# A depthwise convolution moved to TensorE as 64x32 tap matrices, its group norm in that layout, and a new order of the mixer

## The chip, the cores and the metric

The kernel runs on one core of one Trainium2 chip. A core has five engines with their own instruction queues, each worked off strictly in order: TensorE (PE in the profile, its weight loads PEld), VectorE (DVE), ScalarE (ACT), GpSimd (POOL) and SyncE (SP). SP issues all of this kernel's transfers between DRAM and on-chip memory. The metric is device time in microseconds, the median of the runs.

## The reference

One layer on 1024 tokens of 1024 features, in float32. The token mixer projects the normed input to 3072 columns. The first 1024 make a convolution group, the rest an HGRN2 group of four heads:

```python
def _conv_mixer(u_val, u_gate, w_dw, b_dw, gn_gain, gn_bias):
    u = u_val * jax.nn.sigmoid(u_gate)                    # 512 channels
    y = lax.conv_general_dilated(u, w_dw[:, None, :], padding=[(30, 0)],
                                 feature_group_count=512) + b_dw   # 31 causal taps a channel
    # group norm over 8 groups of 64 channels, per token
    return jax.nn.silu(yf * gn_gain + gn_bias)

h = _rms(x, g_pre_mix) * (1.0 + sc_m) + sh_m
p = h @ w_in + b_in
cv = _conv_mixer(p[..., :512], p[..., 512:1024], ...)
hg = _hgrn2(q, fl, i, g, lb, g_out)    # columns 1024 to 3071, 512 each
y = jnp.concatenate([cv, hg], axis=-1) @ w_out
x = x + gt_m * _rms(y, g_post_mix)
```

The channel mixer follows: a norm, an up projection to 4096, squared ReLU, a down projection, a norm and a residual.

## The kernel before

All tiles are 128 partitions wide. A big product is made of three float32r products (high part by high, high by low, low by high), so one column tile of the input projection (128 of the 3072 columns, all 1024 tokens) costs 8 x 3 x 2 = 48 products of 512 columns. A float32 product that is not split appears as two records in the trace.

A class `Weave` sets the order. Streams (Python generators) yield when they would have to wait; `Weave` keeps an estimated clock for each engine, and emits a stream's next instructions when their inputs should be ready. The order on every engine is therefore fixed when the program is built, by the cost formulas in lines 251 to 254.

The stages: an opening (`start`) loads and norms x, computes the first modulation vectors and the first three column tiles (`FIRST`, tiles pf). Then `mixer` (line 1076) runs the other column tiles in the order of `ORDER`, and whatever hangs on a finished tile is woven in between. Then `out_proj`, in which tiles of `EARLY` come first for six of the eight token tiles, and `LATE` after; then the channel mixer (`up`, `down`).

The column tiles are numbered: 0 to 3 conv values, 4 to 7 conv gates, 8 to 11 queries, 12 to 15 forget gates, 16 to 19 the heads' values, 20 to 23 output gates. All but 16 to 19 come out with channels on partitions and tokens along the row; `v_mm` (line 851) computes the heads' values with tokens on partitions, in products of 256 columns.

The convolution has one channel tile of 128 channels at a time. `conv_near` (line 667) runs 20 of the 31 taps on VectorE, each a multiply and add over a whole row into the tile cacc. `conv_far` (line 640) does the other 11 taps on GpSimd, with part of the multiplications on ScalarE. `conv_norm` (line 685) transposes the sum on TensorE (cpt) to tokens on partitions, norms groups of 64 channels, and transposes back (cpb).

Each head runs `head_att` (line 778): seven levels, in each of which TensorE makes a product (pl), VectorE scales three tiles and writes a masked part into the tile att. There is one att tile, so a head starts its levels when the head before has used it up (`att_turn`). `head_state` (to_nat's tn, pS) and `head_out` (po, pot) follow.

Weights arrive by `Loads`: SP loads 512 KB into a stage, ScalarE and VectorE or GpSimd split it. `gate_rows` and `ffn_cols` compute later modulation vectors from in_wada_n, mostly on VectorE.

Of the kernel before, what the change touches and what calls it, by code (L numbers as in the profile page):

```python
# [21 lines left out]
PADW = TAPS - 1  # L22
FF = 4096
NFF = FF // P
NSLOT = 53
# [3 lines left out]
V_BIN, V_BDW, V_GNG, V_GNB, V_GHG, V_LB0, V_LB1, V_GPF, V_WDW = 48, 72, 76, 80, 84, 88, 92, 96, 104  # L29
V_N = V_WDW + 4 * TAPS  # L30
# [7 lines left out]
FIRST = (4, 0, 12)  # L38
ORDER = (5, 8, 13, 9, 1, 6, 16, 2, 7, 14, 21, 10, 20, 3, 15, 18, 23, 11, 22)
# [9 lines left out]
POOL_TAPS, ACT_OF, ACT_TAPS = 11, 2, 1  # L49


EARLY, LATE = (0, 4, 2, 5, 1, 6), (3, 7)
# [3 lines left out]
R0, STAGE, WRING = 12, 3, 6  # L56
SPARE, WOSPARE, HRES = 5, 4, 2
# [5 lines left out]
XRANK, MRANK, RMODS, RFAR, RNEAR, RLOAD, RNORM = 0, 1, 7, 6, 9, 3.5, 1.5  # L63
# [3 lines left out]
class Slots:  # L67
# [3 lines left out]
    def __init__(self, pool, n):  # L71
        self.pool, self.free = pool, list(range(n))
# [3 lines left out]

    def room(self, n):
        return lambda: len(self.free) >= n
# [5 lines left out]
class Slot:  # L84
    def __init__(self, owner, i, dtype):
        self.owner, self.i = owner, i
        t = owner.pool.tile([P, 1024], dtype, tag=f"s{i}", name=f"s{i}", bufs=1)
        if dtype == F32:
            self.f = t
        else:  # L90
            self.r = t

    def release(self):
        self.owner.free.append(self.i)


class Ring:
# [7 lines left out]
    def room(self, n=1):  # L105
        def enough():
            more = n - len(self.items)
            return more <= 0 or (len(self.items) + len(self.lent) + more <= self.n
                                 and len(self.slots.free) >= more + self.spare)
        return enough  # L110

    def next(self):
        self.lent.append(self.items.pop(0) if self.items else self.slots.new(self.dtype))
        assert len(self.items) + len(self.lent) <= self.n
        return self.lent[-1]

    def give(self, item=None):

        item = item or self.lent[0]
        self.lent.remove(item)  # L120
        self.items.append(item)
# [46 lines left out]
class Weave:  # L168
# [16 lines left out]
    def engine(self, eng, key, cost):  # L185
        weave = self

        class Timed:
            def __getattr__(self, name):
                op = getattr(eng, name)  # L190

                def call(*a, **k):
                    weave.spend(key, cost(name, free_size(a[name == "reduce_sum"] if a else k["out"])))
# [53 lines left out]
def block_kernel(ctx: ExitStack, tc: tile.TileContext, x, vecs, masks, rows, vrow, wada_t, wada_n,  # L247
                 win0, win, winv, wout, wup, wdn, out):
# [17 lines left out]
    slots = Slots(big, NSLOT)  # L266
# [6 lines left out]
    def tiny(name, cols=1):  # L273
        return small.tile([P, 8], F32, tag="tiny", name=name, bufs=16)[:, 0:cols]
# [27 lines left out]
    def split(src, hi, lo):  # L302
# [4 lines left out]
        if max(wv.t["G"], wv.now) + n / 460 <= max(wv.t["V"], wv.now) + n / 960 + LO_G:  # L307
# [17 lines left out]
    mhalf = const.tile([P, 8], F32, name="mhalf")  # L325
# [49 lines left out]
    def x_load(n):  # L375
        xn[n] = new()
# [191 lines left out]
    def rest():  # L568
        yield lambda: len(mod_loads) == 4
        srcs = []  # L570
        for j in ORDER:
            srcs += [winv[(j - 16) // 2, i] for i in range(2)] if 16 <= j < 20 else [win[j]]
# [32 lines left out]
    def put_mix(kt, half, fn):  # L605
# [9 lines left out]
        marks.t["mix", kt, half] = wv.now  # L615


    def tap(j, s):
        return col(V_WDW + j * TAPS + PADW - s)

    convs = [dict() for _ in range(4)]
    heads = [dict() for _ in range(4)]

    def conv_gate(j, ps):
        yield room(1)
        u = convs[j]["u"] = new()
        A.activation(u.f, ps, AF.Sigmoid, bias=bcol(4 + j))
        mm.done(ps, "A")
        yield

    def conv_val(j, ps):
        u = convs[j]["u"]
        yield after("A")
        V.scalar_tensor_tensor(u.f, ps, bcol(j), u.f, ALU.add, ALU.mult)
        mm.done(ps, "V")
        yield after("V")
        wv.add(conv_far(j), RFAR)
        wv.add(conv_near(j), RNEAR)

    def conv_far(j):  # L640

        c = convs[j]
        nd = TAPS - POOL_TAPS
        yield room(SPARE + 2)
        c["pacc"] = new()
# [1192 lines left out]
```

## Time and profile before

| what | value |
|---|---|
| median of three runs | 1155.27 us (1154.88 to 1155.27) |
| the profiled execution, its own time | 1161.52 us |
| its span, from the first to the last instruction | 1159.7 us |
| mean granted TensorE clock | 0.971 |
| transfers that SP issues | 353 |

How to read the profile's rows: a group of instructions has its line, engine, operation, the tile written and the tiles read, the shapes and the count, then busy microseconds and the mean duration in nanoseconds, then the idle time of its engine just before it with what ended it. Most operations go through one recording helper (line 194, line 1731 for products), so the tile names tell them apart: s is any of the 53 big tiles. A row of the timeline has the start, the duration, and what ran. A row of the stages has, behind the length, the busy time of each engine with its number of instructions, then the mean granted clock, the busy share of the 16 DMA engines, and GB/s.

### The profile page before, as it was taken

How to read it: one execution, taken by the hardware profiler on the slowest of the kernel's cores; microseconds unless marked ns; L12 is line 12 of the kernel's file. 1: busy time of each engine (PE TensorE's matmuls, PEld its weight loads, DVE VectorE, ACT ScalarE, POOL GpSimd, SP SyncE). 2: the span in 40 equal slices, each digit the busy share in tenths (PEclk: the TensorE clock that was granted, in tenths of full speed). 3: DMA queues.
4: the chain of work that ended last, by engine and by line, in shares of the span. 5: the costliest groups of instructions: out<-in, count | busy, mean ns of one | idle time of the engine just before them, and what ended most of it. 6: DMA issues, size and time to landing. Idle time of an engine off the chain costs nothing.

```text
span 1159.7 us, 14360 instructions
## 1 busy us (share of the span) xinstructions
PE 1090.5 (94%) x5606; PEld 909.5 (78%) x5606; DVE 845.0 (73%) x798; ACT 491.7 (42%) x691; POOL 479.6 (41%) x348
## 2 busy tenths in 40 slices
PE   3899879899998999978999999999999999999996
PEld 3787769787797788857888888888888888888885
DVE  5968988899999986464754986432356969996942
ACT  5643133323433353557544233566543434444520
POOL 6527778756688682484200232223400001304301
PEclk6899889989999999989999999999999999999999
DMA  9423213322311020355467774423666866674801
GB/s 371 165 65 109 74 54 110 127 80 85 92 37 37 26 85 1 117 210 200 145 256 276 293 263 164 135 76 133 220 254 228 319 225 231 246 262 158 323 22 73
DMA packets 50899, 183.96 MB, mean 159 GB/s; under 512 B 5648, under 2 KB 5904, under 8 KB 50832
## 3 DMA queue, kind: packets, MB, share of 16 engines
q1 hardware_dynamic: 50832, 183.05, 44.5%
q8 instruction: 44, 0.72, 0.3%
q14 instruction: 23, 0.19, 0.0%
HBM read 149.47 MB, written 33.55 MB: 158 GB/s over the span
## 4 chain that ended last, share of the span: by engine, by line
PE 54%; DVE 1%; POOL 0%; ACT 0%; DMA 0%; issue 0%; DVEq 0%; POOLq 0%; ACTq 0%
PE pup L1731 26%; PE al L1731 15%; PE be L1731 11%; PE pout L1731 1%; PE pt L1735 1%; DVE s L194 1%; POOL s L194 0%; ACT junk L194 0%; DMA x2d<-s 0%; PE pg L1731 0%; DVEq L1834 0%; POOLq L1834 0%; POOL last_ss L194 0%; POOL fr L194 0%; ACTq L1834 0%
## 5 line engine op out<-in xcount | busy, mean ns | idle before, releaser
L194 POOL TENSOR_TENSOR s<-s,s 128x1024 fp32r<-128x1024 f32 (+9 forms) x164 | 303.7, 1866 | 479.5 <-ACT s L194 443.6
L194 DVE TENSOR_TENSOR s<-s,s 128x1024 fp32r<-128x1024 f32 (+3 forms) x333 | 413.9, 1282 | 80.5 <-ACT s L194 56.1
L194 ACT ACTIVATE s<-s 128x1024 fp32r<-128x1024 f32 (+4 forms) x317 | 298.4, 972 | 298.9 <-DVE s L194 192.1
L1731 PE MATMUL pup<-s,s 128*128 128x512 f32 x1344 | 309.1, 391 | 0.0
L1731 PEld LDWEIGHTS pup<-s,s 128*128 128x128 f32 x1344 | 252.4, 188 | 52.1
L1731 PE MATMUL pj<-s,s 128*128 128x512 f32 (+1 forms) x1200 | 252.1, 366 | 0.0
L1731 PEld LDWEIGHTS pj<-s,s 128*128 128x128 f32 x1200 | 202.4, 193 | 33.0 <-ACT s L194 0.3
L1731 PE MATMUL al<-s,s 128*128 128x512 f32 x768 | 175.6, 390 | 3.1 <-DVE s L194 3.1
L1731 PEld LDWEIGHTS al<-s,s 128*128 128x128 f32 x768 | 143.9, 188 | 34.2 <-DVE s L194 4.3
L1731 PE MATMUL be<-s,s 128*128 128x512 f32 x576 | 131.0, 389 | 0.0
L1731 PEld LDWEIGHTS be<-s,s 128*128 128x128 f32 x576 | 108.1, 188 | 22.5
L1731 PE MATMUL pout<-s,s 128*128 128x512 f32 x384 | 96.4, 401 | 8.4 <-DVE s L194 8.3
L194 DVE SCALAR_TENSOR_TENSOR cacc<-s,vec,cacc 128x1023 f32<-128x1023 f32 (+18 forms) x76 | 96.9, 1275 | 1.1
L1731 PEld LDWEIGHTS pout<-s,s 128*128 128x128 f32 x384 | 71.1, 191 | 23.8 <-DVE s L194 9.2
L194 DVE SCALAR_TENSOR_TENSOR s<-s,c_act,s 128x1024 f32<-128x1024 f32 (+1 forms) x48 | 68.6, 1430 | 19.4 <-DMA s<-in_wada_n 18.0
L194 DVE SCALAR_TENSOR_TENSOR s<-pup,s 128x1024 f32<-128x1024 f32 x16 | 19.6, 1225 | 53.3 <-PE pup L1731 50.4
L194 DVE TENSOR_TENSOR s<-pup,s 128x1024 f32<-128x1024 f32 x24 | 29.3, 1222 | 40.0 <-PE pup L1731 40.0
L194 ACT ACTIVATE s<-s,vec 128x512 f32<-128x512 f32 (+5 forms) x40 | 28.3, 710 | 58.4 <-POOL s L194 58.3
L1731 PEld LDWEIGHTS pl<-s,s 128*16 128x16 f32 (+3 forms) x640 | 34.0, 137 | 21.9 <-issue 15.9
L1731 PE MATMUL pl<-s,s 128*16 128x16 f32 (+3 forms) x640 | 35.9, 222 | 14.8 <-DVE s L194 12.7
L1731 PE MATMUL pf<-s,s 128*128 128x512 f32 x144 | 41.3, 429 | 5.2 <-DVE s L194 3.7
L194 POOL TENSOR_SCALAR s<-s,vec 128x512 f32<-128x512 f32 (+6 forms) x44 | 45.3, 1031 | 0.0
(119 smaller groups left out, 757.1 us busy)
## 6 DMA issues: line engine op xcount, KB each, us to landing
s<-in_wdn SPq DMA_DIRECT2D x72, 512.0 KB, 5.2
s<-in_wup SPq DMA_DIRECT2D x56, 512.0 KB, 5.6
s<-in_wada_n SPq DMA_DIRECT2D x32, 512.0 KB, 3.5
s<-in_win SPq DMA_DIRECT2D x17, 512.0 KB, 3.6
s<-in_x SPq DMA_DIRECT2D x16, 512.0 KB, 6.4
s<-in_wada_t SPq DMA_DIRECT2D x16, 512.0 KB, 9.8
u<-s SPq DMA_DIRECT2D x16, 512.0 KB, 2.9
s<-u SPq DMA_DIRECT2D x16, 512.0 KB, 4.5
```

The lines of the kernel that those rows point to most:

```text
L194: return op(*a, **k)
L1731: return self.te.matmul(out, lhsT=lhsT, rhs=rhs, **k)
L1735: return self.te.transpose(out, in_, identity)
```

## The change

The gate and value columns of the convolution group (G, U) and the heads' values (V) are now all computed with tokens on partitions (`t_mm`): four steps each of 48 products with 512 moving columns. `t_gate` adds the bias and takes the sigmoid, `t_val` adds the bias, multiplies on GpSimd, and SP stores the product to a DRAM tile `udram`, behind 32 rows of zeros.

`conv_input` reads it back into one block tile, `wide`, of four slots. The tokens are cut into 32 blocks of 32; a block's column holds the 64 rows from 32 before the block to its end (row 0 is replaced by ones, which carry the bias). Channels are taken in two halves, each as two groups of rows (partitions 0 to 63 and 64 to 127), so a half takes two reads of 31 rows and two of 32. Then `conv_mm` issues 256 products for each half in two bursts: the stationary operand is the channel's 64x32 tap matrix (made on the host, loaded as in_toep), the moving one its 32 blocks. The result has tokens on partitions again; `conv_evac` copies it out, `conv_norm` norms 1024 columns at once, and `conv_out` turns it back with products by the identity (cpb), which ends in the out projection's input.

Beside this: two attention tiles, so two heads' levels may run at the same time; `FIRST` and `ORDER` bring the first two heads forward, then V, G, U, then the other two heads; `EARLY` and `LATE` of the out projection change; the modulation columns are computed before the gate rows; the ring of split weights has 12 tiles until the last of G, U, V is done and 6 after; the planner's cost formulas for VectorE, ScalarE, GpSimd and products are new.

```diff
-FIRST = (4, 0, 12)
-ORDER = (5, 8, 13, 9, 1, 6, 16, 2, 7, 14, 21, 10, 20, 3, 15, 18, 23, 11, 22)
+TGROUPS = 'GUV'
+FIRST = (12, 8, 13)
+ORDER = (9, 20, 'V0', 'V1', 'V2', 'V3', 'G0', 'G1', 'G2', 'G3', 21, 'U0', 'U1', 'U2', 'U3', 14, 10, 22, 15, 11, 23)
...
-EARLY, LATE = (0, 4, 2, 5, 1, 6), (3, 7)
+EARLY, LATE = (0, 1, 2, 3, 4, 5), (6, 7)
...
-    V = wv.engine(nc.vector, "V", lambda op, n: (0.13 if "scalar" in op else 0.07) + n / 960)
-    A = wv.engine(nc.scalar, "A", lambda op, n: 0.17 + n / 1190)
-    G = wv.engine(nc.gpsimd, "G", lambda op, n: 0.1 + n / (1000 if op == "tensor_scalar" else 460))
+    V = wv.engine(nc.vector, "V", lambda op, n: 0.16 + n / 930)
+    A = wv.engine(nc.scalar, "A", lambda op, n: 0.22 + n / 1190)
+    G = wv.engine(nc.gpsimd, "G", lambda op, n: 0.55 + n / (1350 if op == "tensor_scalar" else 520))
...
-        for s in range(0, TAPS - POOL_TAPS):
-            yield idle("V", NEAR)
-            if s == 0:
-                V.tensor_scalar(acc, uf, tap(j, 0), col(V_BDW + j), ALU.mult, ALU.add)
-            else:
-                V.scalar_tensor_tensor(acc[:, s:], uf[:, 0:T - s], tap(j, s), acc[:, s:], ALU.mult, ALU.add)
...
+    def t_val(s, ps):
+        yield room(1)
+        u = new()
+        V.tensor_tensor(u.f.rearrange("p (a c) -> p a c", c=512), ps.rearrange("p (a c) -> p a c", c=512),
+                        crow_s.f[:, None, H1].broadcast_to([P, 2, 512]), ALU.add)
+        mm.done(ps, "V")
+        yield after("V")
+        G.tensor_tensor(u.f, u.f, sig[s].f, ALU.mult)
+        yield after("G")
+        r0 = CB + 256 * s
+        S.dma_start(udram[r0:r0 + 256, :].rearrange("(a p) c -> p a c", p=P), u.f.rearrange("p (a c) -> p a c", c=512))
...
+    def conv_input():
+        yield slots.gone
+        w = slots.wide().rearrange("p (b c) -> p b c", c=P)
+        for r in range(2):
+            S.dma_start(w[64 * r:64 * r + 1, 0, :], ones[0:1, :])
+            nc.sync.dma_start(w[64 * r:64 * r + 1, 1:, :], ones[1:CB, :])
+        for p in range(2):
+            yield room(4)
+            toeps = [new() for _ in range(4)]
+            for c in range(4):
+                S.dma_start(toeps[c].f, toep[p, c])
+            for r in range(2):
+                for a, n in ((1, CB - 1), (CB, CB)):
+                    src = udram[a:a + T, (2 * p + r) * P:(2 * p + r + 1) * P].rearrange("(b i) c -> i b c", i=CB)
+                    nc.sync.dma_start(w[64 * r + a:64 * r + a + n, :, :], src[0:n])
+                wv.spend("S", 3.0)
+            yield wv.t["S"] + DLAT
+            yield from conv_mm(p, w, toeps)
...
+    def conv_mm(p, w, toeps):
+        for q in range(2):
+            yield acc.free
+            ps = acc.take(ps_acc("cv"))
+            for i in range(16):
+                m = 16 * q + i
+                for c in range(4):
+                    for r in range(2):
+                        rows = slice(64 * r, 64 * r + 64)
+                        TE.matmul(ps[CB * c:CB * c + CB, 512 * r + CB * i:512 * r + CB * i + CB],
+                                  lhsT=toeps[c].f[rows, CB * m:CB * m + CB], rhs=w[rows, :, CB * c + m],
+                                  start=True, stop=True, us=0.03)
...
     def head_att(j):
-        yield lambda: att_turn[0] == j
+        yield lambda: att_turn[0] >= j - 1
         hd = heads[j]
+        att = atts[j % 2]
...
-    def v_mm(j0):
...
+    def t_mm(kind, s):
+        if s == 0:
+            yield loads[0].has(4)
+            tws[:] = [loads[0].get() for _ in range(4)]
+        yield mm.free
+        ps = ps2("pt" + kind)
+        for k in range(KT):
+            w = tws[k // 2]
+            for q in range(2):
+                tsl = slice((2 * s % 4 + q) * P, (2 * s % 4 + q + 1) * P)
+                mm_half(TE, ps[:, HALF[q]], [t[:, tsl] for t in h_halves(k)[s // 2]],
+                        [t[:, HALF[k % 2]] for t in w], k == 0, k == KT - 1)
```

Where instructions stand. On SP, before, this is the end of the mixer's loads: in_win are a column tile's weights, in_wout the out projection's.

```order
L194 DMA s_762<-in_win 128x1024
L194 DMA s_217<-in_win 128x1024
L194 DMA s_762<-in_wout 128x1024
L194 DMA s_217<-in_wout 128x1024
L194 DMA s_3171<-in_wout 128x1024
```

On SP, now, behind the last store to udram: the ones for the second group of rows, the first half's tap tiles (in_toep) and the first two of its four reads into wide.

```order
L233 DMA wide<-ones 1x16x8
L709 DMA wide<-ones 1x31x128
L233 DMA s_2125<-in_toep 128x1024
L233 DMA s_2126<-in_toep 128x1024
L233 DMA s_2127<-in_toep 128x1024
L233 DMA s_2128<-in_toep 128x1024
L718 DMA wide<-udram 31x32x128
L718 DMA wide<-udram 32x32x128
```

The row of 31 and the row of 32 repeat for the second group of rows, and after a load of in_rows and one of in_win the whole group from in_toep on repeats for the second half of the channels. Before, no transfer of SP has other than 128 rows.

On PE, before, this is where the first channel tile's convolution comes back: pj are projection tiles, pg a gate row, cpt the transposes of the convolution's sum, among products of 256 columns for the heads' values.

```order
L1731 MATMUL pj_1153<-s_107,s_634 128x512 x2
L1731 MATMUL pj_1153<-s_106,s_635 128x512 x2
L1731 MATMUL pj_1153<-s_108,s_634 128x512 x2
L1731 MATMUL pj_1153<-s_109,s_634 128x512 x2
L1731 MATMUL pj_1153<-s_108,s_635 128x512 x2
L1731 MATMUL pg<-s_1188,ones_r 128x512
L1731 MATMUL pg<-s_1189,ones_r 128x512
L1735 MATMUL cpt<-msk,s_712 128x128 x4
L1731 MATMUL pj_1275<-s_501,s_94 128x256
```

On PE, now, the end of the two column tiles (14 and 10) that follow U's last step, and the first tap products (cv), two for each of the four tap tiles in turn.

```order
L1835 MATMUL pj_2169<-s_109,s_762 128x512 x2
L1835 MATMUL pj_2169<-s_111,s_761 128x512 x2
L1835 MATMUL pj_2169<-s_112,s_761 128x512 x2
L1835 MATMUL pj_2169<-s_111,s_762 128x512 x2
L1835 MATMUL cv<-wide,s_2125 32x32 x2
L1835 MATMUL cv<-wide,s_2126 32x32 x2
L1835 MATMUL cv<-wide,s_2127 32x32 x2
L1835 MATMUL cv<-wide,s_2128 32x32 x2
```

Between U's last step and the first cv stand 96 projection products; after the first burst of 128 tap products come two of pg and 6 of pj, then the second burst, then two of pg and 60 of pj, then the second half's first burst, 12 of pj and its second. Nothing of the convolution stands on PE before this place.

More of the change, by code (lines that the diff above doesn't have):

```diff
@@ L614, in put_mix @@
         yield from split(full, hi.r[:, sl], lo.r[:, sl])
[L615 to L621, printed above, removed]
+        for n in range(4):
+            marks.t["mix", kt, half * 4 + n] = wv.now
     heads = [dict() for _ in range(4)]
[L624 to L634, printed above, removed]
+    udram = dram.tile([CB + T, 512], F32, name="udram")
+    crow_s = new()
+    S.dma_start(crow_s.f, crow.broadcast_to([P, 1024]))
+    sig = [None] * 4
+    ys = [None, None]
+    u_rows = [0]
+    def t_gate(s, ps):
+        sig[s] = slots.new_last()
+        V.tensor_tensor(sig[s].f.rearrange("p (a c) -> p a c", c=512), ps.rearrange("p (a c) -> p a c", c=512),
+                        crow_s.f[:, None, H0].broadcast_to([P, 2, 512]), ALU.add)
@@ new lines, in block_kernel, with conv_evac @@
+    acc = Banks(wv, 1)
+    def conv_evac(p, q, ps):
+        pv = ps.rearrange("p (r i b) -> p r i b", r=2, i=16)
+        if q == 0:
+            yield room(2)
+            ys[p] = [new(), new()]
+        yield lambda: ys[p]
+        for s in range(2):
+            yv = ys[p][s].f.rearrange("t (b r q i) -> t q r i b", r=2, q=2, i=16)
+            for r in range(2):
+                A.activation(yv[:, q, r], pv[:, r, :, 16 * s:16 * s + 16], AF.Copy)
+        acc.done(ps, "A")
+        yield after("A")
+        if q:
+            for s in range(2):
+                wv.add(conv_norm(p, s), RNORM)
@@ new lines, in block_kernel, with conv_out @@
+    normed = {}
+    def conv_out(s):
+        yield room(2)
+        z, sz = new(), new()
+        for h in range(2):
+            yield aux_free
+            pb = ps1("cpb")
+            for b in range(4):
+                bb = (s % 2) * 8 + 4 * h + b
+                for p in range(2):
+                    TE.matmul(pb[64 * p:64 * p + 64, b * P:(b + 1) * P], lhsT=ys[p][s // 2].f[:, bb * 64:bb * 64 + 64],
+                              rhs=ident, start=True, stop=True, us=0.11)
+            yield after("PE", 0.2)
+            pv = pb.rearrange("p (b c i) -> p c b i", c=4, i=CB)
+            zv = z.f[:, HALF[h]].rearrange("p (c b i) -> p c b i", c=4, i=CB)
+            for c in range(4):
+                A.activation(zv[:, c], pv[:, c], AF.Identity, bias=col(V_GNB + c), scale=col(V_GNG + c))
+            done1(pb, "A")
+        A.activation(sz.f, z.f, AF.Sigmoid)
+        yield after("A")
+        V.tensor_tensor(z.f, z.f, sz.f, ALU.mult)
+        sz.release()
+        yield after("V", 0)
+        yield room(2)
+        hi, lo = mix[s % 2, s // 2] = pair()
+        yield from split(z.f, hi.r, lo.r)
+        z.release()
+        for n in 2 * s, 2 * s + 1:
+            for k in range(4):
+                marks.t["mix", k, n] = wv.now
@@ L885, in head_state @@
     def head_state(j):
         hd = heads[j]
-        yield lambda: ("vh", 0) in hd and ("vh", 1) in hd
+        yield lambda: all(("vh", s) in hd for s in range(4))
         v, f = hd["v"].f, hd["f"].f
@@ L1008, in gate_rows @@
         acc.release()
[L1009 to L1010 removed]
+        gs = new()
+        g = gs.f
         yield ring.room()
@@ L1065, in load_wo @@
     def load_wo(k):
-        yield lambda: len(slots.free) >= WOSPARE + 2 and bool(stage.room()())
+        yield lambda: slots.left() >= WOSPARE + 2 and bool(stage.room()())
         hi, lo = pair()
```

319 lines of the change are left out of this document (161 added, 158 removed).

## The prediction

> **What bounds the kernel now.** I read the page's first part, then the busy times by stage, then what the TensorE waited for.
>
> ```profile
> PE 1090.5 (94%) x5606; PEld 909.5 (78%) x5606; DVE 845.0 (73%) x798; ACT 491.7 (42%) x691; POOL 479.6 (41%) x348
> ...
> core 0: us, PE busy (x) PEld busy (x) DVE busy (x) ACT busy (x) POOL busy (x), PEclk, DMA share, GB/s
> 0.00:76.68 76.68, 55.44 (x263) 45.11 (x263) 51.70 (x89) 43.53 (x81) 36.84 (x48) 0.82 0.60 227
> 76.68:554.84 478.16, 439.98 (x2726) 373.01 (x2725) 396.77 (x398) 190.28 (x342) 322.57 (x238) 0.96 0.26 88
> 554.84:1159.70 604.86, 595.11 (x2623) 491.40 (x2621) 396.49 (x313) 257.92 (x269) 120.21 (x62) 1.00 0.57 206
> ```
>
> PE is busy 94% of the span, so this is a TensorE kernel almost everywhere. The stages are the opening, then everything from the first later projection (76.68) to the steady up projection (554.84), then the rest of the channel mixer. The change lies in the second. There PE is idle 478.16 - 439.98 = 38.2 us, and at a mean clock of 0.96 some 0.04 x 478 = 19 us more go into slow cycles. So at most about 57 us can be won. What those waits are:
>
> ```profile
> PE pl L1731 <- DVE s L194: 16.9, 12, 3.5
> PE pout L1731 <- DVE s L194: 8.3, 1, 8.3
> PE pt L1735 <- POOL s L194: 3.8, 1, 3.8
> PE po L1731 <- DVE s L194: 2.9, 2, 2.7
> PE pot L1735 <- ACT s L194: 2.5, 2, 1.9
> PE pl L1731 <- DVE gsf L194: 2.0, 1, 2.0
> PE pg L1731 <- DVE s L194: 1.3, 1, 1.3
> ```
>
> The columns are total us, times, longest. Mostly a head's next level (pl) waits for VectorE, which in this stage is busy 396.8 of 478 us, largely with convolution taps. The waits inside the mixer (all but pout and pt) come to 25.6 us.
>
> **What is removed.** The taps on VectorE and GpSimd, and the conv's transposes:
>
> ```profile
> L194 DVE SCALAR_TENSOR_TENSOR cacc<-s,vec,cacc 128x1023 f32<-128x1023 f32 (+18 forms) x76 | 96.9, 1275 | 1.1
> ...
> L194 POOL TENSOR_TENSOR s<-s,s 128x512 f32<-128x512 f32 x48 | 73.5, 1532 | 14.4 <-ACT s L194 10.5 <-DVE s L194 2.1
> ...
> L1735 PE MATMUL cpb<-msk,s 128*128 128x128 f32 x32 | 4.9, 274 | 0.0
> L1735 PE MATMUL cpt<-msk,s 128*128 128x128 f32 x32 | 4.7, 274 | 0.0
> ```
>
> VectorE sheds 97 us, GpSimd 80 additions, twenty for each of four channel tiles, of some 1.5 us by the row's mean (120 us), PE 9.6 us of transposes. VectorE and GpSimd are off the path except where a head's level waits for them, so their saving counts only through those waits. VectorE gets back some 20 us: eight reads of a projection's result of 1.22 us (the first row below), sixteen of a quarter that size, and group norm on 1024 columns.
>
> ```profile
> L194 DVE TENSOR_TENSOR s<-pup,s 128x1024 f32<-128x1024 f32 x24 | 29.3, 1222 | 40.0 <-PE pup L1731 40.0
> L194 POOL TENSOR_TENSOR s<-s,s 128x1024 f32<-128x1024 f32 x4 | 11.2, 2798 | 18.0 <-DVE s L194 18.0
> ```
>
> With two attention tiles, two heads' levels alternate, and each level has projection work of another head's step before it. I let the 25.6 us of mixer waits shrink to 5, half of pout's 8.3 stay, pt's 3.8 stay, and 15 of the 19 us of slow clock go, since a slow stretch follows a wait. Gain: 20.6 + 4 + 15 = 40 us. Bounds: 57 if nothing waits, 20 if half of it stays. The later order of the modulation loads, the two weight-ring sizes and the out projection's new EARLY are covered by the same PE work; without that cover they are part of the low bound.
>
> **What PE gets.** Rates first:
>
> ```profile
> 338.43 8.88 PE L1731 MATMUL pj<-s,s 128*128 128x256 f32 x72
> ...
> 405.01 3.51 PE L1731 MATMUL po<-s,s 128*128 128x128 f32 x30
> ...
> 442.40 0.70 PE L1731 MATMUL pl<-s,s 128*16 128x16 f32 x64
> 443.03 0.66 PE L1735 MATMUL cpt<-msk,s 128*128 128x128 f32 x4
> ...
> 446.84 0.70 PE L1731 MATMUL pl<-s,s 128*32 128x32 f32 x32
> 447.47 4.40 PE L1731 MATMUL pout<-s,s 128*128 128x512 f32 x18
> ...
> 451.80 1.15 PE L1731 MATMUL pl<-s,s 128*64 128x64 f32 x16
> 452.87 1.65 PE L1731 MATMUL pout<-s,s 128*128 128x512 f32 x6
> ...
> 476.98 27.48 PE L1731 MATMUL pout<-s,s 128*128 128x512 f32 x120
> ```
>
> A 512-column product costs 27.48/120 = 0.229 us, a 256-column one 8.88/72 = 0.123. The value projection turns 384 of the latter into 192 of the former: 47.4 - 44.0 = 3.4 us less. Gate and value columns of the conv group keep 384 products of 512 columns.
>
> The tap products, 512 with 32 stationary and 32 moving columns, are not in the trace. The nearest are pl's (a float32 product is two records): 32 of 16 columns take 443.03 - 442.40 = 0.63 us, 0.020 each, on four 32-row strips of the result in turn; 16 of 32 columns 0.63 us, 0.039 each, on two strips; 8 of 64 columns 1.07 us, 0.134 each. The tap products use four strips and two halves of the rows, so I take 0.03, 15 us in all; bounds 10 (0.020) and 69 (0.134). The 64 products that turn the conv back (cpb) cost between a transpose, 4.9/32 = 0.153, and a po, 3.51/15 = 0.234: 10 to 15 us, I take 11. PE's sum: -3.4 - 9.6 + 15 + 11 = **+13 us** (7 to 71). Without the new wait, the change is worth 40 - 13 = 27 us.
>
> **The new wait.** cv, the first tap product, stands in PE's queue after 96 projection products. It needs the block tile "wide", which SP reads back from DRAM: for each half of the channels two reads of 31 partitions x 32 x 128 and two of 32. Everything behind cv on PE waits with it. How the queue cuts a transfer:
>
> ```profile
> DMA packets 50899, 183.96 MB, mean 159 GB/s; under 512 B 5648, under 2 KB 5904, under 8 KB 50832
> ...
> u<-s SPq DMA_DIRECT2D x16, 512.0 KB, 2.9
> ...
> vec<-in_vecs SPq DMA_DIRECT2D x1, 114.0 KB, 2.1
> ...
> 20.00:40.00 20.00, 14.80 (x63) 11.16 (x64) 16.69 (x25) 10.63 (x21) 16.18 (x21) 0.71 1.00 397
> ```
>
> The issues in the DMA view add up to 353, all of 128 rows. 353 x 128 = 45184 row packets and 353 x 16 = 5648 tiny ones make exactly the queue's 50832. So a transfer is cut by rows into 16 equal shares, each closed by a tiny packet. 31 rows have no equal shares but 31 or one, and there are 16 engines: I expect one engine to move the whole 31 x 32 x 512 B = 508 KB. The last row has all 16 engines busy (share 1.00) at 397 GB/s, 24.8 GB/s each. By bytes one such read takes d = 508/24.8 = 20.5 us. Its 992 packets of 512 B are smaller than any big transfer's here. From vec (8 packets of 912 B per engine, 2.1 us) to u<-s (8 of 4096 B, 2.9 us) a packet grows 0.1 us for 3184 B, 0.13 us for 4096; one engine's full packet at 24.8 GB/s lasts 0.165, which leaves some 0.036 fixed, so 0.052 for 512 B and d = 52. If a small packet cost as much as a full one, d were 164; but vec's 2.1 us, less some 1.6 in which nothing moves (below), leave only 0.06 us for each of its packets, which bounds d at about 60. Spread over 16 engines d is 1.3. I take **d = 28**, nearer to the byte end, because the other is a difference of two noisy landings.
>
> The Trainium skill, "DMA: Bandwidth & Descriptors", section "Why a DMA increments its semaphore by 16 and not by 1", says that the number of engines is the largest up to 16 that divides the slowest dimension of both sides, and that 127 partitions get a single engine. The count of 5648 agrees with it for 128 rows; no run so far shows 31. By it the sum is the forecast's, and if it did not hold, that of rival (1).
>
> The price, from the end of the last value product at 0: VectorE's add 1.2, GpSimd's product 2.8, then four 512 KB tap tiles at 397 GB/s, 5.3: the reads start at 9.3, with the store (2.9) landed by then. Two reads on one engine and some 1.6 us to land (2.9 less 1.3 of moving): ready at 2d + 11. PE arrives at 96 x 0.229 = 22.0: a stall of 2d - 11. The second half reads into the same tile and must wait for cv's second burst: 2 x 3.8 + 0.5 + 6 x 0.229 = 9.5 us after the first; ready at 9.5 + 2d + 1.6. PE's cover is 60 products, so it arrives at 9.5 + 0.5 + 13.7 = 23.7: a stall of 2d - 12.6. Together 4d - 23.6 = 88 us at d = 28. The out projection now starts with the four conv tiles, whose group norm is about a dozen operations of some 1.2 us behind the last tap burst; 114 projection products (26 us) stand between on PE and cover it. Two gaps as long as these also restart the clock cold:
>
> ```profile
> 512.72 2.93 PE L1731 MATMUL pout<-s,s 128*128 128x512 f32 x6 [8.26 <-DVE s L194]
> ```
>
> Six products took 2.93 instead of 1.38 us, so 1.5 us each, 3 together.
>
> **The sum** goes against the profiled execution's own 1161.5 us (span 1159.7): 1161.5 - 27 + 88 + 3 = 1225.5. The median of the runs is 1155.3, 0.54% lower: **1219 us**. The break-even lies at 4d - 20.6 = 27, d = 12 us: as soon as two engines share a read evenly (10 us) the change wins.
>
> **The rivals.**
> (1) The reads are spread over the engines. Then four reads of 1.3 us make the first half ready at 9.3 + 5.2 + 1.6 = 16.1, before PE at 22.0, and the second at 9.5 + 5.2 + 1.6 = 16.3, before 23.7: nothing stalls, and it is 1161.5 - 27 = 1134.5, or 1128 us: faster. For it: every transfer of the trace is spread. Against: all of them have 128 rows. Chance 0.20; its own range 1110 to 1145.
> (2) Spread, but the alternating heads still wait: 25 of the 40 us do not come, 1153 us. For it: each level still needs three VectorE operations and a mask before the next. Against: VectorE has a quarter less to do. Chance 0.05.
> (3) Spread, but the array does not overlap the tap products: 0.134 instead of 0.03 each, 54 us more, 1182 us. For it: half-width pl costs that. Against: pl of 16 and 32 columns. Chance 0.05.
> The forecast, one engine, has 0.70; its own range goes from d = 20.5 with the whole 40 us won and no extra PE work (1161.5 - 40 + 58 + 3, 1176) to d = 45 with 13 won (1161.5 - 13 + 156 + 3, about 1300).
>
> **How the numbers follow.** Faster by over 0.2% (which is about what a measurement of this kernel tells from no change): 0.20 of (1), 0.03 of (2). Same: 0.02 of (2). Slower: 0.70 + 0.05. The range from 1118 to 1290 takes in the forecast's but its far tail, and two thirds of (1): some 0.13 is left out.
>
> **What would show it.** The tiny packets of the DMA line: 16 for each spread transfer and one for each read of 31 rows. In the waits: cv waiting twice for a DMA of wide, 45 and 43 us, and those reads landing 28 and 56 us after issue. The tap bursts of 128 taking 3.8 us each. pl's 16.9 us on VectorE down to a few. If cv waits for nothing, my d is wrong and (1) holds; if cv runs for 17 us per burst, (3).

## The result, and the profile after

The changed kernel takes **1284.05 us** (median of 4 runs, 1281.47 to 1287.83) against 1155.27 us before: ratio 1.1107, 95% interval 1.1067 to 1.1147. It is slower, as forecast, and inside the range, but by 129 us where 64 were forecast.

The page of the changed kernel, its busy line, the granted TensorE clock in tenths (40 equal slices of 32 us), its DMA line and a queue of instructions (packets, MB, share):

```profile
PE 1107.0 (86%) x6508; PEld 915.2 (71%) x6508; DVE 720.7 (56%) x717; ACT 471.3 (37%) x671; POOL 289.6 (23%) x198
...
PEclk6999999999558578899999999999999999999999
...
DMA packets 61597, 195.04 MB, mean 152 GB/s; under 512 B 6134, under 2 KB 14388, under 8 KB 61524
...
q8 instruction: 51, 0.84, 0.3%
```

VectorE shed 124 us (845.0 to 720.7) and GpSimd 190 (479.6 to 289.6), and yet TensorE is busy for 86% of the span instead of 94%. TensorE's idle time went from 1159.7 - 1090.5 = 69.2 to 1281.5 - 1107.0 = 174.5 us. Busy times by stage:

```profile
core 0: us, PE busy (x) PEld busy (x) DVE busy (x) ACT busy (x) POOL busy (x), PEclk, DMA share, GB/s
0.00:79.00 79.00, 57.47 (x268) 45.94 (x268) 50.60 (x87) 43.77 (x82) 40.09 (x50) 0.83 0.59 220
79.00:677.69 598.69, 455.37 (x3623) 378.37 (x3623) 270.44 (x319) 169.63 (x321) 125.39 (x84) 0.87 0.28 88
677.69:1281.50 603.81, 594.21 (x2621) 490.92 (x2619) 399.69 (x311) 257.94 (x270) 124.12 (x64) 1.00 0.59 207
```

The opening and the last stage are nearly as before (they took 76.7 and 604.9 us). The stage between took 478.2 and takes 598.7 us: 120.5 of the 121.8 us lost lie there. What TensorE waits for in it (columns as before: total us, times, longest):

```profile
PE cv L1835 <- DMA wide<-udram: 82.5, 3, 32.4
PE cv L1835 <- issue: 37.0, 5, 28.3
...
PE pl L1835 <- DVE s L233: 12.0, 6, 4.6
PE pout L1835 <- DVE s L233: 4.4, 1, 4.4
```

The tap products wait for 82.5 + 37.0 = 119.5 us. All other idle time is 174.5 - 119.5 = 55.0 us, 14.2 less than before, and busy time is 16.5 us more: 119.5 - 14.2 + 16.5 = 121.8, the growth of the span. So without the waits of cv the change would still not have won anything. The timeline of TensorE around the taps (start, us, engine, what, count, and in brackets the wait ahead and what ended it):

```profile
288.59 21.92 PE L1835 MATMUL pj<-s,s 128*128 128x512 f32 x96
338.78 0.28 PE L1835 MATMUL cv<-wide,s 64*32 64x32 f32 x2 [28.27 <-issue]
371.50 2.01 PE L1835 MATMUL cv<-wide,s 64*32 64x32 f32 x170 [32.44 <-DMA wide<-udram]
376.86 1.14 PE L1835 MATMUL cv<-wide,s 64*32 64x32 f32 x84 [3.35 <-issue]
...
386.13 13.79 PE L1835 MATMUL pj<-s,s 128*128 128x512 f32 x60
418.63 0.28 PE L1835 MATMUL cv<-wide,s 64*32 64x32 f32 x2 [18.71 <-DMA wide<-udram]
450.22 2.59 PE L1835 MATMUL cv<-wide,s 64*32 64x32 f32 x226 [31.31 <-DMA wide<-udram]
454.43 0.51 PE L1835 MATMUL cv<-wide,s 64*32 64x32 f32 x28 [1.61 <-issue]
```

Each half waits twice: its first product (two records) needs rows 0 to 63 of the block tile, the next rows 64 to 127. The four big waits are 110.7 us; the first is put down to issue, but in the run with divided reads below the wait at the same place is put down to the reads. The other four (3.35, 1.61 and two more of 1.54 and 2.25) stand in the middle of a burst, whose first products have already read from all rows and all four tap tiles: 8.75 us. And what SP issues there:

```profile
301.29 60.46 SPq L718 DMA_DIRECT2D wide<-udram x4
...
385.64 55.87 SPq L718 DMA_DIRECT2D wide<-udram x4
```

The two reads of 31 rows of a half land one after the other. From 301.29 to 338.78 are 37.5 us, less 5.3 for the tap tiles queued ahead (2 MB at 397 GB/s) 32.2; then 371.50 - 338.78 = 32.7; in the second half, counted from 385.64, 33.0 and 31.6. That is **d = 32.4 us** for a read of 31 rows, in the mean. SP itself stands still for most of it.

### The profile page after: what moved, and what is told of

Read it like the earlier page. It is cut to its first block, busy times and chain, and to the rows that moved or that the text cites. A ratio compares the mean times of both kernels' runs of the same rounds, so it can differ in the third digit from the quotient of the medians.

```text
span 1281.5 us, 15966 instructions
## 1 busy us (share of the span) xinstructions
PE 1107.0 (86%) x6508; PEld 915.2 (71%) x6508; DVE 720.7 (56%) x717; ACT 471.3 (37%) x671; POOL 289.6 (23%) x198
## 2 busy tenths in 40 slices
DMA packets 61597, 195.04 MB, mean 152 GB/s; under 512 B 6134, under 2 KB 14388, under 8 KB 61524
## 3 DMA queue, kind: packets, MB, share of 16 engines
q1 hardware_dynamic: 61524, 194.03, 43.8%
## 4 chain that ended last, share of the span: by engine, by line
PE 70%; DMA 10%; DVE 8%; SPq 5%; issue 3%; POOL 2%; ACT 2%; DVEq 0%; POOLq 0%; ACTq 0%
PE pup L1835 23%; PE al L1835 14%; PE be L1835 10%; DVE s L233 8%; DMA wide<-udram 6%; PE pout L1835 5%; SPq L718 5%; PE pj L1835 4%; PE ptG L1835 3%; PE ptV L1835 2%; PE pl L1835 2%; DMA s<-in_wada_n 2%; POOL s L233 2%; PE pf L1835 1%; ACT s L233 1%
## 5 line engine op out<-in xcount | busy, mean ns | idle before, releaser
L233 ACT ACTIVATE s<-s 128x1024 fp32r<-128x1024 f32 (+2 forms) x317 | 304.5, 993 | 375.0 <-DVE s L233 202.7
L233 POOL TENSOR_TENSOR s<-s,s 128x1024 fp32r<-128x1024 f32 (+3 forms) x85 | 191.0, 2254 | 714.6 <-ACT s L233 514.4
L1835 PE MATMUL cv<-wide,s 64*32 64x32 f32 x1024 | 12.8, 245 | 119.5 <-DMA wide<-udram 82.5
L1835 PE MATMUL pj<-s,s 128*128 128x512 f32 x432 | 106.1, 405 | 0.0
L1835 PEld LDWEIGHTS cv<-wide,s 64*32 64x32 f32 x1024 | 11.5, 124 | 121.8 <-issue 121.4
L1835 PEld LDWEIGHTS pj<-s,s 128*128 128x128 f32 x432 | 84.3, 197 | 19.2 <-issue 0.7
L233 DVE SCALAR_TENSOR_TENSOR s<-s,c_act,s 128x1024 f32<-128x1024 f32 (+1 forms) x48 | 56.5, 1177 | 45.3 <-DMA s<-in_wada_n 43.6
L233 ACT ACTIVATE s<-cv 128x256 f32<-128x256 f32 x16 | 7.9, 651 | 141.0 <-PE cv L1835 141.0
L233 DVE SCALAR_TENSOR_TENSOR s<-pj,vec,s 128x1024 f32<-128x1024 f32 x7 | 9.0, 1281 | 87.9 <-ACT s L233 87.9
L233 DVE TENSOR_TENSOR s<-pup,s 128x1024 f32<-128x1024 f32 x24 | 29.3, 1222 | 46.0 <-PE pup L1835 45.8
L1835 PE MATMUL ptV<-s,s 128*128 128x512 f32 x192 | 47.3, 396 | 0.0
```

Source lines behind the costliest of these rows:

```text
L233: return op(*a, **k)
L1835: return self.te.matmul(out, lhsT=lhsT, rhs=rhs, **k)
```

## The experiments

In the last columns of this table: cv's waits for data and those put down to issue, all other idle time of TensorE (span less busy less these two), and its busy time, all in us of the profiled execution. "On" is the kernel that a run was edited from. The ratio compares medians with runs of the kernel before that were made beside each run (1158.9 to 1160.0 us for e1 to e13). The profiled execution is a single one: in e9 it is the shortest of ten, 4.8 us under the median, so differences of a few us between two rows can be chance.

| run | on | ratio to before | span | cv, DMA | cv, issue | other idle | busy |
|---|---|---|---|---|---|---|---|
| before | | 1 | 1159.7 | | | 69.2 | 1090.5 |
| after | before | 1.1107 [1.1067, 1.1147] | 1281.5 | 82.5 | 37.0 | 55.0 | 1107.0 |
| e1 reads 16 + 15 | after | 1.0302 [1.0266, 1.0337] | 1192.7 | 14.8 | 14.5 | 56.5 | 1106.9 |
| e3 16-KB rows | e1 | 1.0184 [1.0159, 1.0208] | 1180.4 | 9.9 | 10.0 | 53.8 | 1106.7 |
| e5 taps in pieces | e3 | 1.0123 [1.0100, 1.0147] | 1175.4 | 11.3 | 5.5 | 55.0 | 1103.6 |
| e6 one head at a time | e3 | 1.0121 [1.0083, 1.0158] | 1170.5 | 10.5 | 9.4 | 47.0 | 1103.6 |
| e8 taps later | e6 | 1.0144 [1.0120, 1.0168] | 1174.5 | 0.9 | 10.3 | 66.7 | 1096.6 |
| e9 taps in halves | e6 | 1.0051 [1.0033, 1.0069] | 1159.8 | 11.1 | 3.2 | 48.0 | 1097.5 |
| e7 both | e6 | 1.0075 [1.0053, 1.0097] | 1163.1 | 1.1 | 1.1 | 58.9 | 1102.0 |
| e10 odd and even rows | e6 | 1.0063 [1.0037, 1.0088] | 1166.2 | 6.8 | 9.6 | 50.2 | 1099.6 |
| e11 halves, odd and even | e9 | 1.0026 [1.0012, 1.0041] | 1160.4 | 6.2 | 3.4 | 51.9 | 1098.9 |
| e12 tap tiles early | e11 | 1.0011 [0.9996, 1.0027] | 1156.2 | 0 | 7.5 | 51.4 | 1097.3 |
| e13 taps in quarters | e12 | 1.0054 [1.0040, 1.0068] | 1162.4 | 1.2 | 1.8 | 54.9 | 1104.5 |

### Does one engine carry a read of 31 rows?

Two edits of the changed kernel. The first divides the 31 rows:

```diff
-                for a, n in ((1, CB - 1), (CB, CB)):
+                for a, n in ((1, 16), (17, 15), (CB, CB)):
```

> The change, with each read of 31 rows cut into one of 16 rows and one of 15, the bytes and the packets unchanged. Theory A (a read of 31 rows runs on one DMA engine): the reads spread over 16 and 15 engines and land within some 8 us, PE's waits for wide fall from 119.5 us to under 10, and the time falls from 1284 to between 1150 and 1175 us. Tiny packets: 16 for each read of 16 and of 32 rows, 15 for each of 15. Theory B (packets of 512 bytes scattered over DRAM are slow in themselves, on however many engines): the same packets wait as long, 1275 to 1290 us. The prediction's rival without the wait would be at 1128 us.

Its tap bursts in the timeline:

```profile
320.96 0.28 PE L1835 MATMUL cv<-wide,s 64*32 64x32 f32 x2 [8.18 <-DMA wide<-udram]
327.81 2.00 PE L1835 MATMUL cv<-wide,s 64*32 64x32 f32 x170 [6.57 <-DMA wide<-udram]
334.11 1.14 PE L1835 MATMUL cv<-wide,s 64*32 64x32 f32 x84 [4.29 <-issue]
```

The same bytes, and 90 us of cv's waits (119.5 to 29.3) are gone. The tiny packets rise from 6134 to 6254: four reads that had one each now have 16 + 15, which is 4 x 30 = 120 more. So the 31 rows were one engine's. But A's waits of under 10 us and its time of 1150 to 1175 us were missed: the kernel takes 1194.36 us, 3% more than before, and the product that needs the last of the half's reads starts 24.4 us after SP issued the first (303.42 to 327.81).

The second edit leaves the 31 rows on one engine, and takes them from 16 KB that lie together in DRAM, so that only the size of the pieces differs (the convolution then gets other tokens' values):

```diff
+                    if n < CB:
+                        src = udram[256 * r:256 * r + 256, :].rearrange("(i a) c -> i (a c)", a=8)
+                        nc.sync.dma_start(w[64 * r + a:64 * r + a + n, :, :].rearrange("i b c -> i (b c)"), src[0:n])
+                        continue
```

> The change, with each read of 31 rows taken from a contiguous part of the DRAM tile (31 rows of 16 KB each, so other tokens' values are convolved): the same bytes in large packets, still 31 rows. If one engine carries it and small packets cost the rest, a read takes 508 KB / 24.8 GB/s = 20.5 us instead of some 32.5, PE's waits for wide are about 70 us, the time about 1236 us. If the engine is as slow with large packets, 32.5 us each and 1284 us stay. If the scattered source were all of the cost (theory B), the waits vanish and the time is 1150 to 1175 us.

```profile
333.13 0.28 PE L1839 MATMUL cv<-wide,s 64*32 64x32 f32 x2 [20.66 <-issue]
357.84 2.00 PE L1839 MATMUL cv<-wide,s 64*32 64x32 f32 x170 [24.42 <-DMA wide<-udram]
...
395.65 0.28 PE L1839 MATMUL cv<-wide,s 64*32 64x32 f32 x2 [10.56 <-DMA wide<-udram]
417.38 2.60 PE L1839 MATMUL cv<-wide,s 64*32 64x32 f32 x226 [21.45 <-DMA wide<-udram]
```

One run: 1249.5 us, where 1236 was expected. A read now takes 357.84 - 333.13 = 24.7, 417.38 - 395.65 = 21.7 and, in the second half's first (issued at 370.83), 24.8 us, near the 20.5 us of the bytes alone. So of the 32.4 us some 22 to 25 come from 508 KB on one engine and 8 to 11 from cutting them into 992 packets of 512 B.

### What do the reads still cost when they are shared?

From here on the conv input lies in DRAM by channel group, token within its block, and block, so that every row read back is one piece of 16 KB:

```diff
-    udram = dram.tile([CB + T, 512], F32, name="udram")
+    udram = dram.tile([P, 33 * P], F32, name="udram")
+    uw = udram.rearrange("(g i) (b c) -> i g b c", g=4, c=P)
...
+        for a in range(2):
+            for b in range(4):
+                S.dma_start(uw[:, :, 1 + 8 * s + 4 * a + b, :],
+                            u.f[CB * b:CB * b + CB, HALF[a]].rearrange("i (g c) -> i g c", c=P))
...
+                for a, n in ((1, 16), (17, 15), (CB, CB)):
+                    i0, b0 = (2 * p + r) * CB + a % CB, a // CB
+                    nc.sync.dma_start(w[64 * r + a:64 * r + a + n, :, :].rearrange("i b c -> i (b c)"),
+                                      udram[i0:i0 + n, b0 * P:b0 * P + T * P // CB])
```

> The conv input is stored in DRAM by channel group, token within the block, block, so that each row that is read back is one piece of 16 KB, and the 31 rows are read as 16 and 15. The stores become pieces of 512 B (32 issues in place of 4). Same computation. Theory A (where 16 engines share a read and its packets are large, nothing of the read-back is left on the path, and heads 2 and 3 waited in the earlier run because cv came later than the order had been planned for): cv waits for DMA fall from 14.8 us in the run with 16 and 15 rows to under 2, the waits inside the heads (pl, pout, cpb, 15 us after the taps there) fall to under 8, and the time is 0.985 to 1.000 of the kernel before. Theory B (the order of the heads after the taps is itself what makes PE wait, whatever the reads do): cv's DMA waits go, but the 15 us after the taps stay, and the ratio is 1.005 to 1.020, 1.0302 less some 15 to 25 us. Theory C (the prediction's gain of 27 us without the wait holds): 0.975 to 0.98.

cv's waits fall by another 9.4 us (29.3 to 19.9), the span by 12.3. Not all of this is the layout's: `Weave` now puts 114 projection products ahead of the first burst instead of 96, some 4 us more cover. The gain of 27 us (C) is not there. A is wrong as well: cv still waits 9.9 us for data. B has the ratio, 1.0184, but not its reason, since the DMA waits did not go. Two edits of later kernels show what cv still waits for. One, on e6 (next part), reads the odd and the even rows in place of the lower and the upper:

```diff
-                for a, n in ((1, 16), (17, 15), (CB, CB)):
+                for a, n, st in ((1, 31, 2), (2, 29, 2), (CB, CB, 1)):
```

> As e6_one_head_at_a_time, but the 31 rows are read as the 16 odd and the 15 even partitions instead of the lower 16 and the upper 15. In e6 the reads of a half (2 MB) landed 15 to 18 us after issue, where 397 GB/s would take 5.3. Theory A (rows that go into neighbouring partitions share a way into SBUF, so that a piece of 16 neighbours is slower than 16 rows spread over 32 partitions): the reads land 3 to 6 us earlier, cv's DMA waits fall from 10.5 to 5 to 7 us and the time by 3 to 6 us. Theory B (the 16-KB rows, or the traffic beside them, set the rate): landing and time as in e6, within 2 us.

The DMA view (issues, size, median us from issue to landing), first of e6, then of e10:

```profile
wide<-udram SPq DMA_DIRECT2D x4, 512.0 KB, 14.4
wide<-udram SPq DMA_DIRECT2D x4, 256.0 KB, 9.3
wide<-udram SPq DMA_DIRECT2D x4, 240.0 KB, 12.8
```

```profile
wide<-udram SPq DMA_DIRECT2D x4, 512.0 KB, 11.2
wide<-udram SPq DMA_DIRECT2D x4, 256.0 KB, 7.5
wide<-udram SPq DMA_DIRECT2D x4, 240.0 KB, 9.1
```

The reads land 2 to 4 us earlier and cv waits 6.8 instead of 10.5 us for them, as A has it. The ratios, 1.0121 and 1.0063, touch in their intervals; 4 us of the difference are busy time, which A does not explain. The edit spreads the rows in DRAM as well as over the partitions, so that the way into SBUF is the cause is not shown.

The other edit, on e9 with these reads (e11, below), loads the first half's four tap tiles after the second value projection instead of ahead of the reads, and tells `Weave` 5 instead of 3 us for each group of reads, so that cv keeps its place:

```diff
+        if u_rows[0] == 2:
+            wv.add(toep_load(), RCONV)
...
-                wv.spend("S", 3.0)
+                wv.spend("S", 5.0)
```

> As e11, and the four tap tiles of the first half (2 MB) are loaded after the second value projection instead of ahead of the reads, so that nothing stands before the reads in the DMA queue; the recorder is told 10 us of SP's time for a half's reads, which leaves 57 projection steps ahead of the first burst, as in e9 and e11. Theory A (the first half's wait is queueing behind the 2 MB of tap tiles, 5.3 us at 397 GB/s): the first half's DMA waits of some 7 us in e10 fall to under 2, and the time is 3 to 6 us under e11's, ratio 0.994 to 0.998, faster than the kernel before. Theory B (the reads' own rate sets it): waits as in e11, time within 2 us.

The reads land after 6.0 to 8.1 us, and cv waits no more for data. A is right about the wait. The time, though, is only 0.15% lower than e11's, with intervals that overlap, and misses A's range. The waits for data fell by 6.2 us, those put down to issue rose by 4.1 (3.4 to 7.5); a new wait at cpb was made up by shorter ones elsewhere (other idle 51.9 to 51.4):

```profile
PE cpb L1856 <- ACT s L233: 9.1, 3, 4.8
PE cv L1856 <- issue: 7.5, 5, 3.1
```

### Do two heads in turn help?

```diff
-        yield lambda: att_turn[0] >= j - 1
+        yield lambda: att_turn[0] >= j
```

> As e3_blocked_layout, but a head's levels start only when the head before is through, as in the kernel before, so that the two attention tiles are never worked on in turn. Theory A (the turn of two heads fills PE's waits for a level, as the prediction has it): 5 to 20 us slower than e3_blocked_layout, with more waiting at pl. Theory B (with VectorE relieved, a head alone hardly waits, and the two heads' operations only get in each other's way on VectorE): equal within 3 us or faster.

e6 is faster than e3: 1.0121 against 1.0184, other idle 47.0 against 53.8 us. The waits of pl on ScalarE fall from 5.8 to 1.6 us, those on VectorE only from 3.0 to 2.6. A, the prediction's view, falls. B's reason, that two heads get in each other's way on VectorE, is not shown, since the shorter waits are ScalarE's; the times show that one head at a time is no worse, and probably better, since the intervals barely part.

### What are the waits in the middle of a burst?

> As e3_blocked_layout, and each burst of 128 tap products is cut in four pieces with projection products between them. Theory A (the gaps of 1.5 to 5.4 us in the middle of a burst, put down to issue, come because 256 records of 12 ns each use up PE's instructions faster than new ones arrive): with 64 records at a time the gaps go, and the run is 4 to 9 us faster than e3_blocked_layout. Theory B (the gaps belong to the reads or to the clock, not to the length of the burst): they are as long as in e3_blocked_layout, and the two times agree within 3 us.

The edit is an empty `yield` after every fourth step of a burst. It put other products between the pieces in some bursts only; the first stayed whole, 152 + 102 records with a gap of 2.24 between. Gaps fell from 10.0 to 5.5 us and the time by 0.6%, within A's 4 to 9 us, but long gaps stayed. That did not decide it. But the timeline of e3 says where the gaps stand:

```profile
326.19 1.82 PE L1839 MATMUL cv<-wide,s 64*32 64x32 f32 x152 [6.24 <-DMA wide<-udram]
330.30 1.30 PE L1839 MATMUL cv<-wide,s 64*32 64x32 f32 x102 [2.29 <-issue]
331.53 3.82 PE L1839 MATMUL pj<-s,s 128*128 128x512 f32 x12
335.29 0.33 PE L1839 MATMUL cv<-wide,s 64*32 64x32 f32 x13
336.56 1.50 PE L1839 MATMUL cv<-wide,s 64*32 64x32 f32 x128 [0.95 <-issue]
340.29 1.46 PE L1839 MATMUL cv<-wide,s 64*32 64x32 f32 x115 [2.23 <-issue]
```

From one gap to the next are 102 + 12 + 13 = 127 records, then 128. In the changed kernel the gaps of a burst stand 255, 383 and 255 records apart, two and three times as far. Each record is a weight load and a product, so 128 are 256 instructions. The page's instruction queue moved 0.84 MB in 51 packets, 16.5 KB each, or 64 B for each of 256. Its packets are TensorE's: 6508 products and as many weight loads are 50.8 times 256, and the 5606 of the kernel before are 43.8 times, where its page has 44 packets. So the bursts were cut in halves of 128 records, this time with a time ahead of which the second half is not placed:

```diff
                                   start=True, stop=True, us=0.03)
+                if i % 8 == 7 and i < 15:
+                    yield wv.now + 0.5
```

> As e6_one_head_at_a_time, but each tap burst of 128 products (256 records) is cut in two, with at least six projection products (1.4 us) and mostly more between the halves. In e3 and e6 the issue gaps stand 127 to 128 records apart (x102, x12, x13 between two of them, then x128), which is 256 instructions with the weight loads, 16 KB at 64 B each, as large as the packets of the instruction queue on the page (51 packets, 0.84 MB). Theory A (PE's instructions come in blocks of 256, and a block of tap products is used up in 1.5 us, faster than the next one comes): the gaps shrink from 9.4 us to under 5, since each block now holds projection products too, and the run is 3 to 6 us faster than e6. Theory B (the gaps come from the length of a burst in some other way, such as the clock or the result banks): no gap is left inside a piece of 128 records, and they do not stand 128 apart. Theory C (they hang on the reads): as in e6.

```profile
321.73 1.53 PE L1841 MATMUL cv<-wide,s 64*32 64x32 f32 x128
326.59 1.52 PE L1841 MATMUL cv<-wide,s 64*32 64x32 f32 x128
...
360.42 0.98 PE L1841 MATMUL cv<-wide,s 64*32 64x32 f32 x75
363.44 0.81 PE L1841 MATMUL cv<-wide,s 64*32 64x32 f32 x53 [2.05 <-issue]
```

cv's gaps fall from 9.4 to 3.2 us (a further 1.3 now stands at pj), and the ratio from 1.0121 to 1.0051, with separate intervals. That is 8 us by the medians, more than A's 3 to 6; busy time, which A does not speak of, is 6.1 us less as well. Inside a piece of 128 there can still be one gap, where a block ends there (x75, x53). A holds, and B, by which a piece has none, falls. With quarters of 64 records:

> As e12_tap_tiles_early, but the bursts are cut in four pieces of 64 records with at least six projection products (1.4 us) between them, the tap tiles are loaded after the third value projection, and a half's reads are told as 6 us, so that 54 projection steps stand ahead of the first burst. Theory A (a block of 256 instructions takes some 3.7 us to come, 1.5 us of taps and a gap of 2.2 us): two pieces and two stretches of projection last 4.3 us and more, so cv's issue waits of 7.5 us go to under 2, and the ratio to the kernel before is 0.994 to 0.998, faster. Theory B (the waits only change their place, as cpb's 9.1 us did in e12): issue waits fall, other waits in the mixer rise, ratio 0.999 to 1.002.

The issue waits fall from 7.5 to 1.8 us, as A says. The time does not follow: it rises to 1.0054, past B's range. Most of the rise is no wait at all: busy time is 7.2 us more (1097.3 to 1104.5), other idle time 3.5. The tap tiles are loaded later here and the bursts stand elsewhere too, so the cut alone was not tried. cpb waits 8.0 us for VectorE in place of 9.1 for ScalarE, and pout 9.0 us in all in place of 5.5:

```profile
PE cpb L1856 <- DVE s L233: 8.0, 2, 6.5
PE pout L1856 <- ACT s L233: 5.3, 1, 5.3
```

### Is it only a matter of where the bursts stand?

Before e11 to e13 came the plain remedy on e6: `wv.spend("S", 7.0)` in place of 3.0, which puts the bursts later in TensorE's order; and then this together with e9's halves.

> As e6_one_head_at_a_time, but the recorder is told that the reads of a half take 14 us of SP's time instead of 6, so that it writes the tap bursts later into PE's order: 18 more projection products and two pd ahead of the first burst (some 5 us), and the second half some 27 products later. Theory A (the 10.5 us in which cv still waits for its reads are only a matter of where the burst stands): the DMA waits of cv fall from 10.5 to under 4 us, the time falls by 5 to 8 us from e6's, the issue waits of 9.4 us stay. Theory B (other work is pushed behind by the same amount, and the heads or the out projection wait instead): cv's DMA waits fall, other waits rise by as much, time within 3 us of e6's.

> Both edits of e8 and e9 on top of e6: the 16-KB layout, one head at a time, reads told at 7 us each, bursts cut in two. If the two are independent, the cv waits of 19.9 us fall to under 7 and the time lies 10 to 14 us under e6's, at 0.998 to 1.004 of the kernel before: what the shorter waits in the heads win (22 us in e6) is then about what PE's added work costs (13 us) and what is left of cv's waits. If other work becomes late instead, 1.005 to 1.012.

Waits of e8:

```profile
PE cv L1839 <- issue: 10.3, 5, 2.8
PE pS L1839 <- ACT s L233: 8.5, 1, 8.5
PE cpb L1839 <- DVE s L233: 4.9, 1, 4.9
PE tn L1843 <- DVE s L233: 4.6, 1, 4.6
...
PE cv L1839 <- DMA wide<-udram: 0.9, 1, 0.9
```

B holds: cv's DMA waits go from 10.5 to 0.9 us, and the other idle time from 47.0 to 66.7. In e7 it is the same with a pd that waits 10.0 us for ScalarE: ratio 1.0075 and not better than e9's 1.0051.

> e9_taps_in_halves with the reads of e10_reads_odd_even: both edits on e6. If they add up, cv's DMA waits (11.1 us in e9) fall by some 4 to 6 us, the issue waits stay near e9's 3.2, and the ratio to the kernel before is 1.0051 less 0.004 to 0.006: 0.999 to 1.001. If the earlier reads only move the wait elsewhere, as with e8, 1.003 to 1.007.

e11, with the reads of e10 on e9, comes to 1.0026: DMA waits 11.1 to 6.2 us, half of the gain expected from the sum, and between the two ranges expected. The best of all, e12, equals the kernel before; none of the runs beats it.

## Why the prediction was right in its direction and wrong in its size

The new wait came as forecast, from the same cause. Three terms of the sum were mis-sized: the wait for the reads (88 us, measured 119.5), TensorE's busy time with its slow clock (1 us more, measured 16.5), and the waits in the heads (24.6 us less, measured 14.2).

**One engine for 31 rows: right.** The forecast named 16 tiny packets for a shared transfer and one for a read of 31 rows. Counted out, of the 379 transfers that SP issues now 373 shared ones x 16 = 5968, six transfers of 31 rows (four reads, two of ones) with one each, and 160 pieces of data that are themselves under 512 B (128 rows of the vectors, 400 B now, and 32 of the first ones row) make 6134. With 16 for each read of 31 rows it would be 6224. The Trainium skill, "DMA: Bandwidth & Descriptors", section "Why a DMA increments its semaphore by 16 and not by 1", gives the largest number of engines up to 16 that divides the count of rows, so one for 31, a prime, and 15 for 15. Here 31 rows agree, with 32.4 us for 508 KB, and 16 and 15 rows agree with 120 more tiny packets. Rivals (1), (2) and (3) all had the reads shared, and fall with it.

**d: mechanism right, size too small.** 28 us was taken, between 20.5 by bytes and 52 by packets; it measured 32.4. The choice leaned to the byte end for being better founded; e2 shows both parts, 22 to 25 us of bytes and 8 to 11 of packets. By 4d - 23.6 the stalls would be 106 us; they were 110.7. The first half's were 60.7 instead of 2d - 11 = 53.8, because its reads could start only some 18 us after the last value product (issued 12.7 us after it, and 5.3 for the tap tiles), not 9.3. The term of 88 us became 119.5 with the 8.75 us in the middle of the bursts, which the forecast did not have. **31.5 us of the miss.**

**Busy time: the clock term was wrong.** 15 of 19 us of slow clock were to come back, less 3 for the clock behind the new gaps; with 13 us of added work, busy time was to grow by 13 - 15 + 3 = 1 us. It grew by 16.5. The granted clock in slices of 4 us gives an estimate of what the slow cycles cost: busy time of a slice times what its clock lacks to 1, since 512-column products slow down with it (six took 2.93 instead of 1.38 us in the prediction's last row). In the middle stage of the kernel before that is 14.9 us; 3.9 of the forecast's 19 lie in idle time and were counted with the waits already. In the changed kernel it is 17.9 (without the taps, which take 12 ns a record at 0.50 as at full clock). Through the long waits the clock stands at 0.50, as the slices of 5 in the row PEclk show, and it is still 0.50 in the first slices behind them. So the new waits took 3 us more, where 15 less 3 were to come back. In e9 and e12, where cv waits less, 7.9 and 9.2 us are left: 6 to 7 came back. The rest of the stage's growth, 12.4 us, is added work, where 13 was forecast: 12.8 for the taps, 11.3 for cpb, -9.6 for the old transposes and -1.4 for the value projection (47.3 for 48.7) by their rows. That this fits so well is partly luck, since the taps cost 2.2 us less and the value projection saved 2.0 less than forecast. **15.5 us of the miss.**

**The waits in the heads: too much.** They were to fall by 24.6 us (20.6 in the mixer and 4 at pout). All idle time but cv's fell by 14.2. pout's 4 came (8.3 to 4.4). pl on VectorE went from 16.9 to 12.0 instead of a few us, although VectorE shed 124 us where 97 less 20 were forecast; so how full VectorE is does not alone set these waits. e3 to e6 point to one reason: the two heads in turn, by which the forecast argued, do not help, and with one at a time the other idle time is 47.0, 22.2 us under the kernel before. **10.4 us of the miss.** The three add up to 57.4; the profiled span grew by 121.8, where 64.0 were forecast, 57.8 less (0.4 of it rounding of the gain).

**The rates of the taps: right, and beside the point.** 256 records take 1.82 + 1.30 = 3.1 us in e3, 0.024 us for each of 128 products, where 0.03 was forecast and rival (3) had 0.134.

**What is left without the reads.** The break-even at d = 12 us rested on a gain of 27 us. With d at a few us (e12: no waits for data) the kernel is equal to the one before. In e12's profile other idle time is 17.8 us less than before, while busy time is 6.8 more and the taps wait 7.5 for their instructions. Rival (1) would have missed as well: the kernel nearest to it is e1, with a ratio of 1.0302, where 1128 us is 0.976, and even e12 comes out some 30 us above it. What stays open is why a wait that was taken away came back in part elsewhere: at pS, tn and cpb in e8, in the taps' waits for instructions in e12, in busy time and at pout in e13. `Weave` lays out the order anew after every edit, and no run held it fixed.

## What to carry to other kernels

Look at the number of rows in the outermost dimension of every new transfer before anything else: 31 rows cost 32 us where 16 + 15 share the engines, and splitting the read in one line of code won 90 us. When a change removes waits, do not book the slow clock as won before asking which waits it adds: here 15 us were booked, and the new waits cost 3 more. When the waits of a planned order are removed one by one, be ready for part of each to come back elsewhere, and price the whole by the sum of busy and idle time.

## What the runs showed of the hardware

- A transfer of 31 rows on one engine holds up the queue that issues it: SP spent 60.46 us on the four issues of a half's reads, where e1's six issues of the same rows took 12.49.
- One engine moved 992 packets of 512 B in 32.4 us, 33 ns each, and the same bytes in rows of 16 KB in 21.7 to 24.8 us.
- 16 neighbouring rows of 16 KB landed later than 16 rows spread over 32 partitions (9.3 against 7.5 us from e6 to e10; 12.8 against 9.1 for 15 rows). The rows were spread in DRAM as well, so the cause is open.
- Tap products took 12 ns a record at a granted clock of 0.50 (170 in 2.01 us, changed kernel, at 371.50) as at 1.00 (126 in 1.51 us, e12, at 308.45).
- TensorE's instructions came in blocks of 256. Tap products use up a block in 1.5 us, and in e3 a gap of 2.23 us follows, 3.73 us from one block's start to the next. That is no fixed rate: the block before, with 12 projection products in it, lasted 6.3 us from 330.30 to 336.56, and 0.95 of this was still a gap. A block of 512-column products alone lasts 29 us (128 x 0.229), and in the kernel before no wait of TensorE is put down to issue. The Trainium skill, "Runtime: NRT & Kernel Launch", section "Instruction fetch mechanics", has the blocks of 16 KB and 256 instructions, and calls crossing one mostly hidden; here the measurement differs, with up to 10.3 us of such gaps in a kernel.
